# One level of Strassen's scheme in both products of a SwiGLU channel mixer, with operand sums through DRAM

## The chip, the core and the metric

The kernel runs on one core of a Trainium2 chip. The metric is device time in microseconds for one execution. The profile comes from one execution taken by the hardware profiler.

## What is computed

An encoder block: two token mixers (a state space model and a long convolution) beside each other, merged by gates, then a channel mixer. One sequence of 1024 tokens, 1024 channels, 2816 hidden channels in the channel mixer, all in float32. The part that matters here is the end:

```python
    merged = gate[:, :, 0] * y_a + gate[:, :, 1] * y_b
    x = x + g1[:, None, :] * (merged @ w_out[i])

    h = _modulate(_rmsnorm(x, norm2_g[i]), sh2, sc2)
    gu = h @ ffn_w_gu[i]
    x = x + g2[:, None, :] * ((jax.nn.silu(gu[..., :D_FF]) * gu[..., D_FF:]) @ ffn_w_down[i])
return _rmsnorm(x, final_g)
```

## The kernel before

Every large product is done in three matmuls. `split` (L134) makes from a float32 tile a rounded part on ACT (a cast, L135) and the rest on DVE or POOL (L136), and `mm3` (L139) adds high x high, high x low and low x high into one bank (L144, L145, L146). A row of the profile with one of these lines says nothing of the place; the tile's name does.

The channel mixer is the last stage. `emit_out` (L1348) multiplies the merged branches by `w_out` for two halves of 512 tokens (`th`), adds to `x1`, takes sums of squares on ACT, and for each half makes the second norm: `inv_rms` on DVE, four diagonal blocks `dg` (L1039), one matmul that spreads them to a row (`rrow`, L1384), 32 transposes (`xT`, L1390), and the scaled and shifted result, split, as `h2T`.

`emit_ffn` (L1408) then goes over the hidden channels in tiles of 128, `FF` = 22 for the gate and 22 for the up half, in four blocks of 6, 6, 6 and 4. For each it loads two weight tiles (`load_w`, L1043: 512 KB, cast on ACT, rest on POOL), does 48 matmuls of 512 columns for each (`gu`), applies Silu on ACT, multiplies on DVE and splits into `act`. After a block it multiplies by the matching rows of `ffn_w_down`: for the first three blocks in quarters of 256 columns (`dn`), for the last in halves of 512 (`dnl`). Each result is scaled by `g2` and added to `x1` on DVE (L1417, L1418). In the last block each tile of 128 tokens is finished at once: a sum of squares on ACT (L1011), the product with `final_g` on POOL (L1473), `inv_rms` on DVE and ACT, a scaling on ACT (L1480) and the store.

What an engine does next is fixed when the program is built: a scheduler puts the instructions of each engine in a row, and each engine works its row in order. All loads and stores of this stage are issued by SP, also in order. A tile from a pool with `bufs` buffers waits for the last reader of the buffer's former content.

## Time and profile before

| | |
|---|---|
| time, median of 3 runs | 1825.1 us (1824.79 to 1826.29) |
| the profiled execution: its time | 1826.97 us |
| the profiled execution: its span | 1825.2 us, 23002 instructions |
| PE busy | 1648.7 us (90%) |
| DVE busy | 1066.9 us (58%) |
| ACT busy | 593.6 us (33%) |
| POOL busy | 746.3 us (41%) |
| DMA | 194.38 MB, mean 106 GB/s |

Busy times are unions over the span of the core. PE and PEld (the load of the stationary operand) overlap. A matmul's own duration in the profile is longer than the distance to the next one, because matmuls are pipelined: what one costs in a row of them is the distance of two starts. Times are counted from the first instruction; the channel mixer's first matmul starts at 1070.03 us.

### The profile page before, as it was taken

The page shows a single profiled execution, that of the slowest core. Times are in us where ns is not written, and L with a number is a line of the kernel's source. Part 1 is how long each engine was busy: PE and PEld are TensorE (multiplying, and loading weights), DVE is VectorE, ACT ScalarE, POOL GpSimd, SP SyncE. Part 2 cuts the span into 40 slices and gives each one's busy share as a digit, 9 for nine tenths or more (in the row PEclk, how much of TensorE's full clock was granted, in tenths as well). Part 3 has the DMA queues.
Part 4 walks back from the last instruction along what each step waited for, and adds up shares of the span by engine and source line. Part 5 has one row for each costly group of instructions (what it writes and reads, how often), then busy time and mean ns, then how long its engine had stood idle before and what let it go on. Part 6 is the DMA issues. An engine that isn't in the chain of part 4 may idle for free.

```text
span 1825.2 us, 23002 instructions
## 1 busy us (share of the span) xinstructions
PE 1648.7 (90%) x8700; PEld 1402.7 (77%) x8700; DVE 1066.9 (58%) x1548; ACT 593.6 (33%) x1037; POOL 746.3 (41%) x509
## 2 busy tenths in 40 slices
PE   6778988998687899998699999999999999999996
PEld 2667767876566777776579997899888998899885
DVE  6889789788999727889877751122211231114127
ACT  5755455443233254222133532110121011110125
POOL 2356545258865347678621222222222222222234
PEclk9898999999888999999899999999999999999998
DMA  9445732433221267754258311111211121112112
GB/s 324 120 132 176 208 110 89 158 89 96 59 74 49 82 178 260 227 175 125 87 164 280 122 53 55 49 40 43 58 47 46 36 58 58 41 36 64 47 53 92
DMA packets 212946, 194.38 MB, mean 106 GB/s; under 512 B 23783, under 2 KB 174143, under 8 KB 211395
## 3 DMA queue, kind: packets, MB, share of 16 engines
q1 hardware_dynamic: 212356, 190.50, 33.8%
q0 software_dynamic: 480, 2.42, 0.4%
q8 instruction: 68, 1.11, 0.3%
q14 instruction: 42, 0.34, 0.1%
HBM read 149.91 MB, written 42.96 MB: 106 GB/s over the span
## 4 chain that ended last, share of the span: by engine, by line
PE 43%; DVE 3%; DMA 2%; ACT 1%; issue 1%; POOL 0%; ACTq 0%; DVEq 0%
PE gu L144 9%; PE gu L145 9%; PE gu L146 9%; PE dn L144 4%; PE dn L146 4%; PE dn L145 4%; DMA wof<-in_w_out_dram 1%; PE wop L144 1%; PE wop L145 1%; PE wop L146 1%; DVE x L1418 1%; DMA gb<-gates 0%; DVE wol L136 0%; DVE ss L1022 0%; PE br L144 0%
## 5 line engine op out<-in xcount | busy, mean ns | idle before, releaser
L136 POOL TENSOR_TENSOR wl<-wf,wh 128x1024 fp32r<-128x1024 f32 (+1 forms) x126 | 285.8, 2269 | 696.5 <-ACT wh L135 667.9
L135 ACT CAST wh<-wf 128x1024 fp32r<-128x1024 f32 (+1 forms) x126 | 118.5, 941 | 607.3 <-issue 191.2
L144 PE MATMUL gu<-h2T,wh 128*128 128x512 f32 x704 | 273.9, 391 | 3.4 <-ACT silu L1432 2.8
L145 PE MATMUL gu<-h2T,wh 128*128 128x512 f32 x704 | 275.0, 391 | 0.0
L146 PE MATMUL gu<-h2T,wl 128*128 128x512 f32 x704 | 274.7, 390 | 0.0
L1433 DVE TENSOR_TENSOR silu<-gu,silu 128x1024 f32<-128x1024 f32 x22 | 26.9, 1224 | 371.8 <-PE gu L146 365.5
L144 PE MATMUL pj<-hT,wh 128*128 128x512 f32 x480 | 197.8, 412 | 9.6 <-ACT cva L1180 8.9
L146 PE MATMUL pj<-hT,wl 128*128 128x512 f32 x480 | 195.7, 408 | 3.0 <-POOL wl L136 3.0
L145 PE MATMUL dn<-wl,act 128*128 128x256 f32 x576 | 162.8, 283 | 0.0
L146 PE MATMUL dn<-wh,act 128*128 128x256 f32 x576 | 162.8, 283 | 0.0
L144 PE MATMUL dn<-wh,act 128*128 128x256 f32 x576 | 161.8, 283 | 0.0
L144 PEld LDWEIGHTS gu<-h2T,wh 128*128 128x128 f32 x704 | 132.4, 188 | 31.4 <-ACT silu L1432 3.2
L146 PEld LDWEIGHTS gu<-h2T,wl 128*128 128x128 f32 x704 | 132.7, 188 | 27.5
L145 PEld LDWEIGHTS gu<-h2T,wh 128*128 128x128 f32 x704 | 132.7, 188 | 27.3
L144 PEld LDWEIGHTS pj<-hT,wh 128*128 128x128 f32 x480 | 95.1, 198 | 28.9 <-ACT cva L1180 9.6
L1417 DVE TENSOR_TENSOR tmp<-dn,g 128x256 f32<-128x256 f32 x96 | 35.9, 414 | 134.7 <-PE dn L146 134.7
L146 PEld LDWEIGHTS pj<-hT,wl 128*128 128x128 f32 x480 | 94.7, 197 | 22.9 <-POOL wl L136 3.8
L145 PEld LDWEIGHTS dn<-wl,act 128*128 128x128 f32 x576 | 110.7, 192 | 0.1
L146 PEld LDWEIGHTS dn<-wh,act 128*128 128x128 f32 x576 | 110.7, 192 | 0.0
L144 PEld LDWEIGHTS dn<-wh,act 128*128 128x128 f32 x576 | 110.1, 192 | 0.1
L145 PE MATMUL pj<-hT,wh 128*128 128x512 f32 x256 | 105.3, 411 | 0.0
L145 PE MATMUL pj<-lT,wh 128*128 128x512 f32 x224 | 90.4, 404 | 0.0
(411 smaller groups left out, 3732.4 us busy)
## 6 DMA issues: line engine op xcount, KB each, us to landing
wf<-in_ffn_w_gu_dram SPq DMA_DIRECT2D x44, 512.0 KB
wf<-in_w_in_dram SPq DMA_DIRECT2D x36, 512.0 KB
ada<-in_ada_w_dram SPq DMA_DIRECT2D x48, 256.0 KB
x<-in_x_dram SPq DMA_DIRECT2D x16, 512.0 KB
kt<-kspec SPq DMA_DIRECT2D x32, 256.0 KB
wof<-in_w_out_dram SPq DMA_DIRECT2D x16, 512.0 KB
wf<-in_ffn_w_down_dram SPq DMA_DIRECT2D x16, 512.0 KB
kspec<-kt SPq DMA_DIRECT2D x28, 256.0 KB
```

The lines of the kernel that those rows point to most:

```text
L135: E.nc.scalar.copy(hi, src)
L136: (lo_eng or E.nc.vector).tensor_tensor(out=lo, in0=src, in1=bc(hi), op=ALU.subtract)
L144: E.nc.tensor.matmul(out=out, lhsT=lh, rhs=rh, start=first, stop=False, skip_group_check=shared)
L145: E.nc.tensor.matmul(out=out, lhsT=lh, rhs=rl, start=False, stop=False, skip_group_check=shared)
L146: E.nc.tensor.matmul(out=out, lhsT=ll, rhs=rh, start=False, stop=last, skip_group_check=shared)
L1417: V.tensor_tensor(out=tmp, in0=acc, in1=E.g2[:, cs], op=ALU.mult)
L1418: V.tensor_tensor(out=x1[t][:, cs], in0=x1[t][:, cs], in1=tmp, op=ALU.add)
L1433: V.tensor_tensor(out=s, in0=pts[1], in1=s, op=ALU.mult)
```

## The change

Both products of the channel mixer are computed with seven block products in place of eight, in Winograd's form of Strassen's scheme. For the first, the stationary operand is the weight (gate above up, in two halves of the 1024 input channels) and the moving one is `h2T` (two halves of channels by two halves of tokens). For the second, the stationary operand is the activation (two halves of tokens by two halves of hidden channels) and the moving one `ffn_w_down`.

`emit_out` ends without the second half's norm; it stores `x1` to DRAM (`E.x1d`). `emit_norm2_end` makes that half's norm and the moving operands B22, T1, T2, T3, T4 of the first product (sums and differences on DVE, each split). `emit_gu` makes 11 passes `j`, each over the hidden tiles `j` and `j + 11`. For each tile, `weights` loads gate and up (`wg`, `wu`) and makes S1 to S4 on DVE, each split into `op`; `gate` is a generator of seven steps, one block product of 12 matmuls each, with results read out of the banks between them; two such generators run in turn. At the end of a pass DVE makes the four sums of the activations that the second product needs, and SP stores seven tiles of 256 KB to DRAM (`E.ad`).

`emit_down` has seven products over 11 `j` each. For each `j` it loads one A tile (`af`, a ring of 4) and one to three tiles of `ffn_w_down` (`bf`, a ring of 8; `t2` has tiles of its own), makes the T operands on DVE, and splits both into `dop`, a ring of 25. Four tiles of 128 tokens take each pair in turn (12 matmuls); in the last product, S4 by B22, all 11 pairs are made first and each tile runs through (33 matmuls). Results are put together on DVE, `x1` is loaded again (`y`), and the end of each tile is as before. PSUM is now one pool of eight banks for the stage.

```diff
-            ss = op.tile([P, 12], F32, tag="ss", name="ss2", bufs=2)
-            V.tensor_reduce(out=ss[:, 0:4], in_=sq, op=ALU.add, axis=mybir.AxisListType.X)
-            dg = diagonals(E, op, "dg", inv_rms(E, ss, 4))
...
+            for i in range(4):
+                nc.sync.dma_start(out=E.x1d[4 * th + i], in_=xs[i])
+            if th:
+                return sq
+            row = norm2_rows(E, rooms(op), ps, "n2", sq)
             for k in range(8):
...
-                hi, lo = E.hT[k, th] = [E.actT.tile([P, 512], F32R, tag="a", name="h2T") for _ in range(2)]
...
-                nc.scalar.activation(out=hi, in_=h, func=ACTF.Identity, bias=shift)
-                V.scalar_tensor_tensor(out=lo, in0=h, scalar=shift, in1=bc(hi), op0=ALU.add, op1=ALU.subtract)
+                h = E.actT.tile([P, 512], F32, tag="a", name="h2")
+                norm2(E, h, xs, k, row, ps, "n2")
+                E.h[k, 0] = h
+                hl = [E.actT.tile([P, 512], F32R, tag="a", name="h2T") for _ in range(2)]
+                split(E, h, *hl)
+                E.B["B11" if k < 4 else "B21"].append(hl)
...
+
+def strassen_a(TT, a11, a12, a21, a22, s1, s2, s3, s4):
+    TT(out=s1, in0=a21, in1=a22, op=ALU.add)
+    TT(out=s2, in0=s1, in1=a11, op=ALU.subtract)
+    TT(out=s3, in0=a11, in1=a21, op=ALU.subtract)
+    TT(out=s4, in0=a12, in1=s2, op=ALU.subtract)
...
+    for k in range(8):
+        h = room("h2", [P, 512])
+        norm2(E, h, x1[4:8], k, row, ps, "b")
+        h2.append(h)
+        if k < 4:
+            t1 = tmp()
+            V.tensor_tensor(out=t1, in0=h, in1=E.h[k, 0], op=ALU.subtract)
+            E.B["T1"].append([mine(), mine()])
+            split(E, t1, *E.B["T1"][k])
+    close()
+    pool = more()
+    for i in range(4):
+        at = (lambda: pool.tile([P, 512], F32R, tag="a", name="h2T")) if i < 2 else mine
+        b22, t3, t2, t4 = h2[i + 4], tmp(), tmp(), tmp()
+        V.tensor_tensor(out=t3, in0=b22, in1=h2[i], op=ALU.subtract)
+        V.tensor_tensor(out=t2, in0=t3, in1=E.h[i, 0], op=ALU.add)
+        for n, src, eng in (("B22", b22, GP), ("T3", t3, V), ("T2", t2, V), ("T4", None, V)):
+            if src is None:
+                src = t4
+                V.tensor_tensor(out=t4, in0=E.h[i + 4, 0], in1=t2, op=ALU.subtract)
+            hl = [at(), at()]
...
+        g = E.wp.tile([P, 8, P], F32, tag="wf", name="wg", bufs=2)
+        up = fp.tile([P, 8, P], F32, tag="wu", name="wu", bufs=2)
+        load(g, P * f)
+        load(up, (FF + f) * P)
...
+        split(E, g, gh, gl, nc.gpsimd)
+        four = lambda h, l, o=0: [(h[:, o + k], l[:, o + k]) for k in range(4)]
+        A["A11"], A["A12"] = four(gh, gl), four(gh, gl, 4)
+        g1, g2, u1, u2 = g[:, 0:4], g[:, 4:8], up[:, 0:4], up[:, 4:8]
+
+        def put(n, src):
+            t = fp.tile([P, 2, 4, P], F32R, tag="op", name="op", bufs=6)
+            split(E, src, t[:, 0], t[:, 1])
+            A[n] = four(t[:, 0], t[:, 1])
+
+        new = lambda: fp.tile([P, 4, P], F32, tag="ws", name="ws", bufs=3)
+        sub = lambda out, a, b: V.tensor_tensor(out=out, in0=a, in1=b, op=ALU.subtract)
+        s1, s2, s4, s3 = new(), new(), new(), new()
+        V.tensor_tensor(out=s1, in0=u1, in1=u2, op=ALU.add)
+        put("S1", s1)
+        sub(s2, s1, g1)
+        sub(s4, g2, s2)
+        put("S4", s4)
...
+        sub(s3, g1, u1)
+        put("S3", s3)
+        put("A22", u2)
...
+        go(X, "A11", "B11", True)
+        p1 = u("p1")
+        nc.scalar.copy(p1, X)
+        yield
...
+        go(Y, "S2", "T2", True)
+        g2 = u("g2")
+        V.tensor_tensor(out=g2, in0=Y, in1=p1, op=ALU.add)
+        V.tensor_tensor(out=g2, in0=Z, in1=g2, op=ALU.add)
+        nc.scalar.activation(out=g2, in_=g2, func=ACTF.Silu)
+        yield
+        go(Y, "S3", "T3", False)
+        a2 = u("a2")
+        V.tensor_tensor(out=a2, in0=Y, in1=p1, op=ALU.add)
...
+        go(Y, "A22", "T4", False)
+        a1 = u("a1")
...
+    for j in range(FH):
+        E.act = []
+        two = [gate(weights(f)) for f in (j, j + FH)]
+        for _ in range(7):
+            for g in two:
+                next(g)
+        (a11, a21), (a12, a22) = E.act[0:2], E.act[2:4]
+        S = [u("S") for _ in range(4)]
+        strassen_a(V.tensor_tensor, a11, a12, a21, a22, *S)
+        for n, t in zip(("A11", "A12", "A22", "S1", "S2", "S3", "S4"), [a11, a12, a22] + S):
+            nc.sync.dma_start(out=E.ad[n][j], in_=t)
...
+    nc.sync.dma_start(out=g2, in_=E.g2d.to_broadcast([P, L]))
+    nc.sync.dma_start(out=fg, in_=d["final_g"].rearrange("(a c) -> a c", a=1).to_broadcast([P, L]))
...
+    def operand(src, eng):
+        t = fp.tile([P, 2, 512], F32R, tag="op", name="dop", bufs=25)
+        split(E, src, t[:, 0], t[:, 1], eng)
+        return t[:, 0], t[:, 1]
+
+    def a(n, j):
+        t = fp.tile([P, 512], F32, tag="af", name="af", bufs=4)
+        nc.sync.dma_start(out=t, in_=E.ad[n][j])
+        return operand(t, V)
...
+        t = fp.tile([P, 512], F32, tag="bf", name="bf", bufs=8)
+        r = (FH * (i - 1) + j) * P
+        nc.sync.dma_start(out=t, in_=d["ffn_w_down"][0, r:r + P, 512 * (h - 1):512 * h])
...
+    def b(n, j):
+        if n[0] == "B":
+            t = load_b(int(n[1]), int(n[2]), j)
+        elif n == "T1":
+            t, o = load_b(1, 2, j), load_b(1, 1, j)
+            TT(out=t, in0=t, in1=o, op=ALU.subtract)
...
+        elif n == "T2":
+            t = t2[j] = fp.tile([P, 512], F32, tag=f"t2{j}", name="t2")
+            r = (FH + j) * P
+            nc.sync.dma_start(out=t, in_=d["ffn_w_down"][0, r:r + P, 512:1024])
+            for m, op in ((2, ALU.subtract), (1, ALU.add)):
+                TT(out=t, in0=t, in1=load_b(1, m, j), op=op)
...
+        return operand(t, GP if j % 3 == 2 else V)
+
+    def product(out, na, nb, start, whole=False):
+
+        ops = []
+        for j in range(FH):
+            ops.append((a(na, j), b(nb, j)))
+            if not whole:
+                for t in range(4):
...
+                    (ah, al), rhs = ops[j]
+                    mm3(E, out[t], [(ah[:, r], al[:, r])], [rhs], start and j == 0, j == FH - 1, True)
+        for t in range(4):
+            if whole:
+                r = slice(P * t, P * t + P)
+                mm3(E, out[t], [(ah[:, r], al[:, r]) for (ah, al), _ in ops], [rhs for _, rhs in ops], start, True, True)
...
+    def done(t, h):
+        sum_sq(E, y[t, h], v("junk"), sq[:, t, h:h + 1])
+        GP.tensor_tensor(out=y[t, h], in0=y[t, h], in1=half(fg, h), op=ALU.mult)
...
+    X, Y = four(), four()
+    for t in product(X, "A11", "B11", True):
+        p1.append(v("p1"))
+        nc.scalar.copy(p1[t], X[t])
+    for t in product(Y, "S2", "T2", True):
+        u2.append(v("u2"))
+        TT(out=u2[t], in0=Y[t], in1=p1[t], op=ALU.add)
...
+    for t in product(Y, "S3", "T3", False):
+        u3.append(v("u3"))
+        TT(out=u3[t], in0=Y[t], in1=p1[t], op=ALU.add)
+        load_y(t, 1)
+        add(t, 1, u2[t], u2[t])
...
+    for t in product(X, "S4", "B22", False, True):
+        add(t, 1, X[t])
+        done(t, 1)
+        finish(t)
...
+            sq = emit_out(E, mm, x1, woA, last_gate)
         wo.close()
-        ps2 = pool(top, "dn", space=PSUM)
-        emit_ffn(E, mm, ps2, x1)
+        sm.close()
+        ps = pool(top, "ff", bufs=8, space=PSUM)
+        with ExitStack() as s0:
+            fp = pool(s0, "ffn")
+            emit_norm2_end(E, fp, ps, x1, sq, sx.close, lambda: pool(right, "T2", bufs=16, side="right"))
+            emit_gu(E, fp, ps)
+        ws.close()
+        right.close()
+        emit_down(E, pool(top, "down"), ps)
```

PE at the start of the channel mixer: `rrow` is the matmul that spreads the second half's norm, `xT` are its transposes, `gu` is the first product. Before:

```order
L144 MATMUL gu<-h2T,wh 128x512
L145 MATMUL gu<-h2T,wh 128x512
L1384 MATMUL rrow<-dg,ones 128x512
L1390 MATMUL xT_9179<-ident,x_7925 128x128
L1390 MATMUL xT_9179<-ident,x_7926 128x128
```

And now, where `wop` is the product with `w_out`:

```order
L146 MATMUL wop<-woh,mT 128x256
L1358 MATMUL rrow<-dg,ones 128x512
L1369 MATMUL xT_9218<-ident,x_7934 128x128
L1369 MATMUL xT_9218<-ident,x_7935 128x128
L1369 MATMUL xT_9218<-ident,x_7936 128x128
```

Before, 38 matmuls of `gu` stand between the last `wop` and `rrow`, and the transposes come in groups between others; now `rrow` and all 32 transposes follow the last `wop`, and `gu` comes after them.

DVE in the same place, now: `Ts` are the sums for T1 to T4, `h2T` the splits of them, `ws` the sums of the first tile's weights (L1512 is S1's), `op` their splits.

```order
L1469 TENSOR_TENSOR Ts_9380<-Ts_9379,h2_8577 128x512
L136 TENSOR_TENSOR h2T_9389<-Ts_9379,h2T_9388 128x512
L1473 TENSOR_TENSOR Ts_9381<-h2_8577,Ts_9380 128x512
L1512 TENSOR_TENSOR ws_9409<-wu_9402 128x512
L136 TENSOR_TENSOR h2T_9393<-Ts_9380,h2T_9392 128x512
L136 TENSOR_TENSOR h2T_9398<-Ts_9381,h2T_9397 128x512
L1510 TENSOR_TENSOR ws_9410<-ws_9409,wg_9401 128x512
L136 TENSOR_TENSOR op_9414<-ws_9409,op_9414 128x512
```

S1 of the very first tile stands behind all sums of the moving operands but the last two splits.

SP between the two products, now: `adS2` to `adS4` are stores of the last pass, `af` and `bf` the first loads of the second product.

```order
L1572 DMA adS2_75<-S_12522 128x512
L1572 DMA adS3_76<-S_12523 128x512
L1572 DMA adS4_77<-S_12524 128x512
L1583 DMA g2r_12544<-g2d_70 128x1024
L1584 DMA fg_12545<-in_final_g_dram 128x1024
L1596 DMA af_12557<-adA11_71 128x512
L1602 DMA bf_12562<-in_ffn_w_down_dram 128x512
L1596 DMA af_12579<-adA11_71 128x512
```

Where before the weight tiles of `emit_ffn` followed one another through the whole stage, the second product's first load now stands behind the last store of the first.

## Rows read from the trace of the kernel before

**Rows 1.** The page, the chain that ended last: shares by line

```profile
PE gu L144 9%; PE gu L145 9%; PE gu L146 9%; PE dn L144 4%; PE dn L146 4%; PE dn L145 4%; DMA wof<-in_w_out_dram 1%; PE wop L144 1%; PE wop L145 1%; PE wop L146 1%; DVE x L1418 1%; DMA gb<-gates 0%; DVE wol L136 0%; DVE ss L1022 0%; PE br L144 0%
```

**Rows 2.** Timeline, start of the mixer: start, duration, engine, line, what

```profile
1070.03 0.39 PE L144 MATMUL gu<-h2T,wh 128*128 128x512 f32 x1
...
1073.19 0.88 DVE L1039 TENSOR_SCALAR dg<-ident,ss 128x128 f32<-128x128 f32 x4
...
1078.66 1.02 PE L1384 MATMUL rrow<-dg,ones 128*128 128x512 f32 x2
...
1080.33 0.75 DVE L1399 SCALAR_TENSOR_TENSOR hk<-xT,mod,rrow 128x512 f32<-128x512 f32 x1 [6.26 <-ACT rrow L1386]
```

**Rows 3.** Timeline, end of the kernel, PE and DVE

```profile
1809.53 0.39 PE L146 MATMUL dnl<-act 128*128 128x512 f32 x1
...
1811.38 0.68 DVE L1417 TENSOR_TENSOR tmp<-dnl,g 128x512 f32<-128x512 f32 x1
...
1814.70 0.68 DVE L1417 TENSOR_TENSOR tmp<-dnl,g 128x512 f32<-128x512 f32 x1
1815.42 0.69 DVE L1418 TENSOR_TENSOR x<-x,tmp 128x512 f32<-128x512 f32 x1
```

**Rows 4.** Busy time in the mixer's stretch, selected by tile: gu, dn, dnl

```profile
1070.00:1809.60 739.60, 482.74 (x2112) 396.98 (x2112) 26.93 (x22) 22.30 (x22) 1.00 0.16 48
...
1070.00:1809.60 739.60, 207.83 (x1728) 207.75 (x1728) 35.86 (x96) 1.00 0.16 48
...
1070.00:1809.60 739.60, 43.36 (x192) 36.05 (x192) 9.64 (x14) 1.00 0.16 48
```

**Rows 5.** Timeline of PE after its one gap in `gu`, and at its steady pace

```profile
1099.26 0.50 PE L144 MATMUL gu<-h2T,wh 128*128 128x512 f32 x1 [2.79 <-ACT silu L1432]
...
1101.44 0.63 PE L144 MATMUL gu<-h2T,wh 128*128 128x512 f32 x1
...
1104.43 0.52 PE L145 MATMUL gu<-h2T,wh 128*128 128x512 f32 x1
...
1105.26 0.39 PE L145 MATMUL gu<-h2T,wh 128*128 128x512 f32 x1
...
1109.79 0.39 PE L144 MATMUL gu<-h2T,wh 128*128 128x512 f32 x1
```

**Rows 6.** Stretches: PE, PEld, DVE, ACT, POOL busy, granted clock, DMA share, GB/s

```profile
1100.00:1110.00 10.00, 9.39 (x34) 7.63 (x35) 2.56 (x2) 1.19 (x2) 2.37 (x1) 0.83 0.37 105
1110.00:1212.00 102.00, 102.00 (x457) 84.74 (x456) 14.07 (x9) 18.90 (x19) 22.21 (x10) 1.00 0.15 44
```

**Rows 7.** The chain in order of time: start, duration, what; eight transposes

```profile
1079.68 0.87 PE xT L1390 x8
```

**Rows 8.** Groups by shape, from 1000 on: count, busy, mean ns, idle before

```profile
L136 POOL TENSOR_TENSOR wl<-wf,wh 128x1024 fp32r<-128x1024 f32 x58 | 139.9, 2413 | 487.2 <-ACT wh L135 487.2
...
L1473 POOL TENSOR_TENSOR yo<-x,fg 128x512 f32<-128x512 f32 x16 | 20.7, 1291 | 19.7 <-DVE ss L1021 10.3 <-DVE x L1418 7.5 <-DVE ss L1022 1.8
L1418 DVE TENSOR_TENSOR x<-x,tmp 128x512 f32<-128x512 f32 x16 | 15.7, 983 | 0.5
...
L135 ACT CAST wh<-wf 128x512 fp32r<-128x512 f32 x12 | 7.4, 620 | 68.9 <-PE dn L146 42.1 <-issue 26.7
```

**Rows 9.** Timeline, POOL and DVE at the same time in the merge

```profile
930.99 1.62 POOL L136 TENSOR_TENSOR wl<-wf,wh 128x512 fp32r<-128x512 f32 x1 [4.50 <-ACT wh L135]
931.38 1.78 DVE L1341 TENSOR_TENSOR gb<-gb,ya 128x512 f32<-128x512 f32 x1
```

**Rows 10.** The chain in order of time: two 256 KB transfers

```profile
962.29 8.15 DMA gb<-gates
...
1000.29 3.49 DMA acc<-acc
```

**Rows 11.** Stretches with the densest transfers, columns as in rows 6

```profile
950.00:975.00 25.00, 22.32 (x119) 18.69 (x119) 17.69 (x26) 6.88 (x11) 1.96 (x2) 1.00 0.83 287
...
1000.00:1025.00 25.00, 25.00 (x210) 24.88 (x209) 15.64 (x28) 11.13 (x27) 6.14 (x4) 1.00 0.58 184
```

More of the change, by code (lines that the diff above doesn't have):

```diff
@@ L1356, in emit_out @@
             xs = x1[4 * th:4 * th + 4]
[L1357 removed]
+            sq = E.cp.tile([P, 4, 4], F32, name="sq")
             for q in range(4):
@@ L1379, in emit_out @@
                     between()
-            ss = op.tile([P, 12], F32, tag="ss", name="ss2", bufs=2)
-            V.tensor_reduce(out=ss[:, 0:4], in_=sq, op=ALU.add, axis=mybir.AxisListType.X)
-            dg = diagonals(E, op, "dg", inv_rms(E, ss, 4))
-            pt = ps.tile([P, 512], F32, tag="n2", name="rrow")
-            nc.tensor.matmul(out=pt, lhsT=E.ones, rhs=dg.rearrange("p a b -> p (a b)"), start=True, stop=True)
-            row = op.tile([P, 512], F32, tag="rrow", name="rrow")
-            nc.scalar.copy(row, pt)
@@ new lines, with emit_norm2_end @@
+FF = 22
+FH = FF // 2
+def strassen_a(TT, a11, a12, a21, a22, s1, s2, s3, s4):
[3 more added lines that the diff above has]
+    TT(out=s4, in0=a12, in1=s2, op=ALU.subtract)
+def emit_norm2_end(E, fp, ps, x1, sq, close, more):
+    nc = E.nc
+    V, GP = nc.vector, nc.gpsimd
+    room = lambda tag, shape: fp.tile(shape, F32, tag="u", name=tag, bufs=NU)
+    row = norm2_rows(E, room, ps, "b", sq)
+    h2 = []
+    mine = lambda: E.actT.tile([P, 512], F32R, tag="a", name="h2T")
+    tmp = lambda: fp.tile([P, 512], F32, tag="ws", name="Ts", bufs=3)
+    for k in range(8):
[9 more added lines that the diff above has]
+    pool = more()
+    for i in range(4):
+        at = (lambda: pool.tile([P, 512], F32R, tag="a", name="h2T")) if i < 2 else mine
[7 more added lines that the diff above has]
+            hl = [at(), at()]
+            split(E, src, *hl, eng)
+            E.B[n].append(hl)
@@ new lines, in gate, with go @@
+    def gate(A):
+        def go(out, a, b, start):
+            mm3(E, out, A[a], E.B[b], start, True, True)
+        X, Y, Z = bank(), bank(), bank()
+        go(X, "A11", "B11", True)
+        p1 = u("p1")
+        nc.scalar.copy(p1, X)
+        yield
+        go(X, "A12", "B21", False)
+        s = u("s1")
+        nc.scalar.activation(out=s, in_=X, func=ACTF.Silu)
+        yield
+        go(Z, "S1", "T1", True)
+        p5 = u("p5")
+        nc.scalar.copy(p5, Z)
+        yield
+        go(Z, "S4", "B22", False)
+        yield
+        go(Y, "S2", "T2", True)
[3 more added lines that the diff above has]
+        nc.scalar.activation(out=g2, in_=g2, func=ACTF.Silu)
+        yield
+        go(Y, "S3", "T3", False)
+        a2 = u("a2")
+        V.tensor_tensor(out=a2, in0=Y, in1=p1, op=ALU.add)
+        V.tensor_tensor(out=a2, in0=a2, in1=p5, op=ALU.add)
+        V.tensor_tensor(out=a2, in0=a2, in1=g2, op=ALU.mult)
+        yield
+        go(Y, "A22", "T4", False)
+        a1 = u("a1")
+        V.tensor_tensor(out=a1, in0=Y, in1=p1, op=ALU.add)
+        V.tensor_tensor(out=a1, in0=a1, in1=s, op=ALU.mult)
+        E.act += [a1, a2]
+        yield
@@ L1498, in hybrid_block @@
         E.acc = D("acc", [4, P, L])
+        E.x1d, E.g2d = D("x1d", [8, P, L]), D("g2d", [1, L])
+        E.ad = {n: D("ad" + n, [FH, P, 512]) for n in ("A11", "A12", "A22", "S1", "S2", "S3", "S4")}
+        E.h, E.B = {}, {n: [] for n in ("B11", "B21", "B22", "T1", "T2", "T3", "T4")}
         E.ya = D("ya", [8, P, L])
```

186 lines of the change are left out of this document (98 added, 88 removed).

## The prediction

> **What bounds the kernel now.** First the chain that ended last [rows 1]: it runs through the matmuls of the channel mixer, `gu` and `dn`; no other engine has a large share in it. Then the mixer's own stretch. Its first `gu` matmul starts at 1070.03 [rows 2], its last `dnl` matmul at 1809.53 [rows 3], and the span ends at 1825.2. By the three rows that select a tile [rows 4] PE's busy time there is 482.74 + 207.83 + 43.36 = 733.9 us of those 739.9: PE is full. The spacing of starts gives the price of one matmul: 20 steps from 1105.26 to 1109.79, so 0.2265 us for 512 columns [rows 5]; the 256-column ones cost 207.83/1728 = 0.120 us [rows 4]. In the same stretch DVE works 14 of 102 us, POOL 22, and the transfers move 44 GB/s [rows 6]. So there is room beside PE, and fewer matmul columns are worth their full price, as long as the new work of DVE and of the transfers stays under PE's shorter time.
>
> **What goes.** Before: 2112 `gu` x 0.2265 + 1728 `dn` x 0.120 + 192 `dnl` x 0.2265 = 478.4 + 207.4 + 43.5 = 729.3 us. After: `emit_gu` issues 11 passes x 2 gates x 7 products x 12 = 1848 matmuls, `emit_down` 7 products x 11 x 4 x 3 = 924, all of 512 columns: 418.6 + 209.3 = 627.9 us. The gain is 101.4 us at most: an eighth of the columns, and 6% on the half-width ones.
>
> **What comes at the start.** PE had 38 `gu` matmuls to do while DVE made `dg` from the last sums of squares. In the new order `rrow` and all 32 transposes stand ahead of the first `gu` matmul, so PE waits from 1070.0 until `dg` is done at 1073.19 + 0.88 [rows 2]: 4.1 us. `rrow` and the transposes cost 1.02 [rows 2] + 4 x 0.87 [rows 7] = 4.5 us, as before. Then 48 matmuls on `A11`, `A12` need only what is ready and last 10.9 us, until 1089.5. The next product needs S1. DVE takes S1's first step (L1512) after 4 `h2` steps and 30 sums, differences and splits for T1 to T4. It can start 1.67 us after `rrow` does, the distance from 1078.66 to 1080.33 [rows 2], at about 1075.8. With 0.75 us for each of the 4 [rows 2] and 0.69 for each 128x512 tensor-tensor alone [rows 3], that is 3.0 + 31 x 0.69 = 24.4 us, to 1100.2. But POOL works in this stretch too: four products with the row, four splits of B22, two weight splits of 2.41 us [rows 8]. Beside a POOL operation of 1.62 us a DVE one took 1.78 instead of 0.69 [rows 9], 1.1 us more; ten such meetings add up to 11 us. So S1 comes between 1100 and 1111; I take 1108, nearer the upper end, since POOL's list is long, and a cast of 0.62 [rows 8]. PE waits 19.2 us here (11 to 22). The rest of this first pass has 27.2 us of PE and some 40 DVE steps of 0.69 = 27.6 us: 3 us more (0 to 8).
>
> The first trace row on this sharing is the 1.78 us one. The Trainium skill, "SBUF — State Buffer", section "SBUF: two separate sides", calls the pair of ports that DVE and GpSimd share an exclusive lock, the loser waiting for the whole instruction; by it each meeting would cost DVE a whole POOL operation, 1.3 us and not 1.1, and the first wait would be some 2 us longer. The trace's 1.1 is below that and decides.
>
> **The ten further passes.** A pass has 168 matmuls, 38.1 us. DVE has 36 steps of 0.69 = 24.8 us, and two POOL splits of 2.41 us beside it; ACT has two casts of 1024 and some 18 of 512 columns, about 13 us at 0.62 for 512 [rows 8]. Both fit. Bank `Y` is read by DVE between two products into it; the other gate's product, 12 x 0.2265 = 2.7 us, is the cover. I take 4 us for all ten (0 to 20: two late reads in each pass).
>
> **Between the products.** SP issues the first load of `emit_down` behind the last store of pass 10, and behind `g2r` and `fg`. From PE's last `gu` matmul: three DVE steps (2.1 us), then about 2.4 MB of stores and loads up to the first pair, then a cast and a split (1.3 us). The transfer is bounded by 3.5 us, a lone 256 KB [rows 10], and by 2.4 MB at 287 GB/s [rows 11], 8.3 us. I take the second, since all is queued at once: 12 us (7 to 15).
>
> **The down stage.** Up to its last pair SP loads 214 x 256 KB + 1 MB = 57.2 MB. At 287 GB/s [rows 11] that is 199 us beside 209.3 us of PE: close, but under. DVE has about 244 tensor-tensors (77 splits of A, 56 of B, 55 sums and differences of weights, 56 on results): 168 us at 0.69, and 37 POOL operations of 1.29 us [rows 8] that cost it up to 1.1 us each, 41 us. Together 209, again PE's time; the ring of 25 `dop` tiles lets the operands run up to 12 pairs (33 us) ahead, which evens out the heavy products (S2·T2, S3·T3, S1·T1). I take 8 us of waits (0 to 30).
>
> **Clock and end.** After a gap of 2.79 us [rows 5] the granted clock fell to 0.83 of full over 10 us [rows 6]: between 1101.44 and 1104.43 seven matmuls took 0.427 us each, the spacing at 1.2 GHz, and cost 1.4 us. I take 4 us for the gaps above (1.4 to 8). The end: from the last tile's `tmp` at 1814.70 to 1825.2 [rows 3], 10.5 us behind the last matmul. Before, DVE, ACT and POOL ran 3.3 us per tile against PE's 2.7, so they trailed PE by 4.8 us there; now a tile of the last product has 33 matmuls, 7.5 us, and nothing trails.
>
> **Sum.** 1070.0 + 4.1 + 4.5 + 418.6 + 19.2 + 3 + 4 + 12 + 209.3 + 8 + 4 + 10.5 = 1767.2 us of span, 58 below 1825.2. The profiled execution took 1826.97 and becomes 1769; the median of the runs, 1825.1, stands beside the span, so the time is 1767.
>
> **The rivals.**
>
> *DVE sets the down stage.* If its 244 steps go at the mean of `x<-x,tmp` beside POOL, 0.983 us [rows 8], they take 240 us, with four `finish` of 3.3 us 253, against 217 in the sum: 1767 + 36 = 1803. For it: POOL splits every third B operand. Against: most steps meet no POOL operation, which is busy 48 us.
>
> *The loads set the down stage* (the one that ends slower). A ring of four `af` tiles turns once per load, cast and split. At 8.15 us for a load, the longest on the chain before [rows 10], that is 9.5/4 = 2.4 us a pair against PE's 2.7. It becomes the bound from a landing of about 9.6 us, and eats the whole gain (66 us over 77 pairs, 3.6 us a pair) from 13 us on. At the 184 GB/s of 1000 to 1025 [rows 11], 57.2 MB take 311 us: 1767 + 94 = 1861. For it: SP is one queue in order, and each load waits for a split of DVE. Against: where the transfers were wanted they ran at 287 GB/s with 0.83 of the engines busy [rows 11].
> Here a page speaks against the change: the Trainium skill, "DMA: Bandwidth & Descriptors", section "Rules for kernel authors", asks for 1 MiB per transfer, and its table under "Bandwidth" has 138 GB/s at 64 KB, 341 at 1 MB; at an estimated 138 for these 256 KB loads the stage would take over 400 us. The trace's 287 GB/s, reached with loads of 256 and 512 KB in flight together, disagrees.
>
> *PE waits at every read of `Y`.* If DVE's queue is behind by more than the cover of 2.7 us in every pass, each of 44 reads shows 0.69 us and a handover, say 1.4 us by two DVE steps: 62 us, 1767 + 58 = 1825, no change.
>
> *All is covered.* S1 at 1100 (8 less), no waits in down (8), none in the passes and the first pass's rest (7), a switch of 7 us (5): 1739.
>
> **Chances.** The forecast (1748 to 1792) 0.57; DVE in down (1792 to 1815) 0.15; all covered (1735 to 1748) 0.13; loads in down 0.09; waits at `Y` 0.06, half of it slower, a third the same. A measurement of this kernel tells about 0.2%, 3.6 us, from no change. Faster 0.86, same 0.02, slower 0.12. The range that leaves out the last two is 1738 to 1812.
>
> **What would show it.** Right: PE's 1848 and 924 matmuls at 0.2265 us; one wait of PE of some 19 us after 48 `gu` matmuls with DVE as the releaser; 11 to 13 us between last `gu` and first `dn`; passes of 38 to 39 us; a down stage of 209 to 225 us. Wrong: gaps in every pass, or PE waiting through the down stage on `dop` with DVE idle (loads) or full (DVE).

## The result, and the profile after

The changed kernel takes 1768.3 us (median of 4 runs, 1766.17 to 1775.56) against 1825.7 before: the ratio is 0.969, 95% interval 0.966 to 0.972. A second set of runs of the same kernel gave 1767.4 (1765.02 to 1769.97), ratio 0.968 (0.966 to 0.969). The forecast was 1767, so it was right in sum. It was not right term by term, and that is the more useful part of what follows.

The page of the first profile after the change: span, PE, DVE and POOL busy, then the chain that ended last by line, which answers to [rows 1].

```profile
span 1773.8 us, 21889 instructions
PE 1566.3 (88%) x7440; PEld 1287.4 (73%) x7440; DVE 1333.7 (75%) x1944; ACT 722.8 (41%) x1331; POOL 708.7 (40%) x484
PE gu L145 8%; PE gu L144 8%; PE gu L146 8%; POOL dop L136 1%; DMA bf<-in_ffn_w_down_dram 1%; DMA wof<-in_w_out_dram 1%; DMA af<-adA 1%; DMA af<-adS 1%; DMA y<-x1d 1%; DVE dop L136 1%; PE dn L144 1%; ACT dop L135 1%; DVE h2T L136 1%; PE dn L145 1%; PE dn L146 1%
```

PE is still what bounds the mixer: `gu` leads the chain. DVE has gone from 58% to 75% of the span; the transfers from 194 to 264 MB.

This first profile comes from the slowest of the four executions. The second profile (1767.3 us of span) stands near the median, so the reading goes by it. Its waits of PE from 1050 us on: who waited for whom, total us, times, longest:

```profile
PE gu L144 <- ACT op L135: 13.4, 1, 13.4
PE dn L144 <- ACT dop L135: 13.2, 1, 13.2
PE rrow L1358 <- DVE dg L1356: 3.9, 1, 3.9
PE gu L146 <- DVE op L136: 0.5, 1, 0.5
PE gu L144 <- ACT p L1531: 0.3, 1, 0.3
```

Three waits make up nearly all of it: for the first S1 (`op`), between the products (`dop`), and for `dg`. In the first profile the same three are there, and 3.9 us more of waits in the second product, by which it is slower. The stretches of the second profile, columns as in [rows 6]:

```profile
1070.00:1082.00 12.00, 8.07 (x42) 6.60 (x41) 6.54 (x17) 4.94 (x11) 2.44 (x2) 0.72 0.54 153
...
1093.00:1107.00 14.00, 0.58 (x2) 0.47 (x2) 14.00 (x23) 8.32 (x15) 5.81 (x2) 0.62 0.00 0
1107.00:1120.00 13.00, 12.35 (x41) 8.90 (x41) 12.74 (x17) 5.58 (x9) 7.10 (x2) 0.75 0.41 122
1120.00:1528.00 408.00, 408.00 (x1757) 330.76 (x1756) 239.26 (x374) 126.95 (x204) 45.80 (x19) 1.00 0.30 94
1528.00:1542.00 14.00, 0.94 (x5) 0.43 (x3) 4.23 (x7) 1.14 (x2) 0.00 (x0) 0.69 0.84 267
1542.00:1560.00 18.00, 17.85 (x69) 14.60 (x70) 9.90 (x15) 8.38 (x15) 2.58 (x2) 0.86 1.05 386
1560.00:1740.00 180.00, 179.94 (x794) 148.72 (x793) 155.00 (x228) 91.15 (x170) 61.72 (x29) 1.00 0.78 267
```

From 1093 to 1107 PE works 0.6 us of 14 while DVE has not one free moment; from 1120 to 1528 PE is full and DVE 59% busy; from 1560 to 1740 PE is full again, DVE 86%. The granted clock is 1.00 in the full stretches and between 0.62 and 0.86 around the three waits.

The terms of the sum beside what this profile shows (us; the third column is worked out from the starts of the first and last matmul of each stage, which are 1074.36 for `rrow`, 1081.12 and 1528.56 for `gu`, 1542.15 and 1754.08 for `dn`):

| term | forecast | measured |
|---|---|---|
| up to PE's wait for `dg` | 1070.0 | 1070.4 |
| wait for `dg` | 4.1 | 3.9 |
| `rrow` and 32 transposes | 4.5 | 6.8 |
| 1848 `gu` | 418.6 | 429.5 |
| wait for S1 | 19.2 | 13.9 |
| rest of the first pass, ten further passes | 7 | 0 |
| between the products | 12 | 13.4 |
| 924 `dn` | 209.3 | 209.5 |
| waits in the down stage | 8 | 0 |
| clock and handovers (4.2 in `gu`, 2.6 in `dn`) | 4 | 6.8 |
| behind the last matmul | 10.5 | 13.0 |
| sum | 1767.2 | 1767.2 |

Seven terms were 20.5 us too low together and four 20.5 us too high.

### The profile page after: what moved, and what is told of

It reads as the page before. It is cut to its first block, busy times and chain, and to the rows that moved or that the text cites. A ratio compares the mean times of both kernels' runs of the same rounds, so it can differ in the third digit from the quotient of the medians.

```text
span 1773.8 us, 21889 instructions
## 1 busy us (share of the span) xinstructions
PE 1566.3 (88%) x7440; PEld 1287.4 (73%) x7440; DVE 1333.7 (75%) x1944; ACT 722.8 (41%) x1331; POOL 708.7 (40%) x484
## 5 line engine op out<-in xcount | busy, mean ns | idle before, releaser
L136 POOL TENSOR_TENSOR wl<-wf,wh 128x1024 fp32r<-128x1024 f32 (+1 forms) x56 | 130.3, 2326 | 162.6 <-ACT wh L135 131.1
L144 PE MATMUL gu<-h2T,op 128*128 128x512 f32 x440 | 174.9, 397 | 13.9 <-ACT op L135 13.9
L136 POOL TENSOR_TENSOR wl<-wg,wh 128x1024 fp32r<-128x1024 f32 x22 | 53.8, 2446 | 317.3 <-ACT wh L135 317.3
L145 PE MATMUL gu<-h2T,op 128*128 128x512 f32 x440 | 174.8, 397 | 0.0
L146 PE MATMUL gu<-h2T,op 128*128 128x512 f32 x440 | 169.7, 396 | 0.5 <-DVE op L136 0.5
L144 PE MATMUL dn<-dop 128*128 128x512 f32 x308 | 114.9, 395 | 14.7 <-ACT dop L135 14.7
L135 ACT CAST op<-ws 128x512 fp32r<-128x512 f32 x88 | 54.3, 620 | 178.4 <-PE gu L146 171.7
L145 PE MATMUL dn<-dop 128*128 128x512 f32 x308 | 121.6, 395 | 2.1 <-DVE dop L136 2.1
L146 PE MATMUL dn<-dop 128*128 128x512 f32 x308 | 121.0, 393 | 0.0
L144 PEld LDWEIGHTS gu<-h2T,op 128*128 128x128 f32 x440 | 83.3, 189 | 34.3 <-ACT op L135 15.0
L136 POOL TENSOR_TENSOR dop<-bf,dop 128x512 fp32r<-128x512 f32 x18 | 42.9, 2383 | 150.6 <-ACT dop L135 72.2
L146 PEld LDWEIGHTS gu<-h2T,op 128*128 128x128 f32 x440 | 83.5, 190 | 20.9 <-DVE op L136 1.3
L145 PEld LDWEIGHTS gu<-h2T,op 128*128 128x128 f32 x440 | 83.5, 190 | 19.3
L136 DVE TENSOR_TENSOR dop<-af,dop 128x512 fp32r<-128x512 f32 x77 | 58.6, 762 | 31.6 <-ACT dop L135 31.3
L144 PEld LDWEIGHTS dn<-dop 128*128 128x128 f32 x308 | 58.5, 190 | 27.7 <-ACT dop L135 15.6
L135 ACT CAST dop<-af 128x512 fp32r<-128x512 f32 x77 | 47.8, 621 | 67.9 <-DMA af<-adA 53.4
```

The costliest lines, as they stand in the source:

```text
L135: E.nc.scalar.copy(hi, src)
L136: (lo_eng or E.nc.vector).tensor_tensor(out=lo, in0=src, in1=bc(hi), op=ALU.subtract)
L144: E.nc.tensor.matmul(out=out, lhsT=lh, rhs=rh, start=first, stop=False, skip_group_check=shared)
L145: E.nc.tensor.matmul(out=out, lhsT=lh, rhs=rl, start=False, stop=False, skip_group_check=shared)
L146: E.nc.tensor.matmul(out=out, lhsT=ll, rhs=rh, start=False, stop=last, skip_group_check=shared)
```

## The experiments

The edits are small, so each is told by the few lines that differ. "The changed kernel" is the one of the diff above; where a stage is compared, it is with its second profile. `thin`, `edge_24_nopool`, `edge_72_rows` and `edge_8_inner` have one execution each (1597.9, 1764.7, 1753.0 and 1766.2 us), and what is said of them is read inside a stage of the trace, not from these times.

### The changed kernel once more

> The changed kernel once more, unaltered. In its first profile a gu matmul cost 0.2324 us (starts from 1170.99 to 1210.03, 168 matmuls) and a dn matmul 0.2267, and that execution took 1775.6 us where three others took 1766 to 1769. Theory A: the slower spacing belongs to that one execution; then this profile, if its time is near 1767, shows gu at about 0.2267 and a first product some 10 us shorter. Theory B: it belongs to the program; then gu is at 0.232 again whatever the time, and the 8 us between the executions are elsewhere.

Measured: 1767.4 us, and `gu` again at 0.2324 us a matmul in each pass (39.0 us for 168), `dn` at 0.2267. Theory B: the spacing belongs to the program. The 6.5 us between the two profiled spans lie nearly all in the second product: 217.8 against 211.9 us from first to last `dn`.

### The pad ahead of the moving operands

By the program's addresses, which no trace shows, the stationary tiles of `gu` start at 192 modulo 256 bytes in the changed kernel and the moving ones at 64; before, both started at 64. A tile that only takes up room stands ahead of the moving operands, and its width says where these start. The change took it from 424 floats to 40. That is 1536 bytes, six times 256, so this line alone leaves the moving tiles where they were modulo 256; it is the stationary ones that came to start elsewhere. The experiment makes the pad 8, so that the moving tiles follow by 128 bytes.

```diff
-            pool(right, "edge", side="right").tile([P, 40], F32, name="edge")
+            pool(right, "edge", side="right").tile([P, 8], F32, name="edge")
```

> The pad tile ahead of the moving operands is 8 floats wide and no longer 40, so that all tiles of that side of SBUF lie 128 bytes elsewhere; nothing else differs. By the program's addresses a stationary tile of gu starts at 192 modulo 256 bytes and a moving one at 64 in the changed kernel; before the change both started at 64, and the tiles of dn all start at 192. Theory A (stationary and moving tiles that start at unlike places modulo 256 slow the pairs of weight load and matmul): gu falls from 0.2324 to 0.2267 us a matmul, 1848 x 0.0057 = 10.5 us, and the time to 1755 to 1759. Theory B (the slower spacing comes from the order of the products, or from what DVE and ACT do beside them): gu stays at 0.232 and the time at 1767.

> Two edits in stretches that the trace tells apart. First, the pad is 24 floats: moving tiles of gu start at 128 modulo 256 bytes against 192 of the stationary ones, 64 apart where the changed kernel has them 128 apart. If only an equal start gives 0.2267 us, gu shows something slower here too (0.229 to 0.233); if 64 apart does no harm, 0.2267. Second, the splits of the second product that POOL made are made by DVE. Theory A (DVE sets the stage only where it shares with POOL): DVE works some 14 us more, dn stays within 4 us of 212, with no wait on POOL. Theory B (POOL relieves DVE where it is the bound): dn grows by 5 to 14 us, with waits on DVE's dop.

> Two edits in stretches that the trace tells apart. First, the pad is 72 floats: moving tiles of gu start at 192 modulo 512 bytes and stationary ones at 448, equal modulo 256 and 256 apart modulo 512; in edge_8 both start at 448 modulo 512. If equal starts modulo 256 are enough, gu is at 0.2267 us a matmul; if they must agree modulo 512, at 0.232 or so. Second, the two rows g2 and final_g (512 KB each as written) are loaded behind the second product's first pairs and no longer ahead of them. Theory A (the gap of 13.6 us between the products is partly transfers that run together, 1 MB at 388 GB/s): it shrinks by 2 to 3 us, to 11. Theory B (SP's issues in order and one transfer's own latency set it): by the two issues, 1 us.

Measured, `edge_8`: 1759.5 us (1755.91 to 1763.77), 7.8 under the changed kernel; the first product is 10.2 us shorter, the gap behind it 1.3 us longer. `edge_24_nopool` and `edge_72_rows` have a second edit each, of which more below. The stretch of 1200 to 1400 us, selected by the tile `gu`: length, then PE's busy time with its count. The changed kernel, pad 40:

```profile
1200.00:1400.00 200.00, 200.00 (x862) 162.17 (x861) 28.20 (x41) 16.05 (x30) 1.00 0.32 102
```

pad 8:

```profile
1200.00:1400.00 200.00, 200.00 (x884) 165.66 (x883) 29.59 (x43) 16.00 (x30) 1.00 0.33 104
```

pad 24:

```profile
1200.00:1400.00 200.00, 200.00 (x859) 161.15 (x858) 27.53 (x40) 16.04 (x30) 1.00 0.32 102
```

pad 72:

```profile
1200.00:1400.00 200.00, 200.00 (x884) 165.62 (x883) 29.81 (x44) 16.00 (x30) 1.00 0.32 102
```

In the same 200 us, PE full and the granted clock at 1.00 in all four, 884 matmuls go through where stationary and moving tiles start at the same place modulo 256 bytes, and 859 to 862 where they start 64 or 128 apart, all by the program's addresses. A pass takes 38.1 us with the pad of 8 and 39.0 with 40; the whole first product 437.2 against 447.4 us. Starts 256 apart (pad 72) do no harm. In all of these runs the fast place of the moving tiles is 192; that it is the equal start that counts, and not that place, rests on the kernel before, with both at 64 and 0.2265 us [rows 5]. So Theory A holds, and the mis-sized `gu` term was not a property of Strassen's scheme but of where its operands lie.

### The wait for S1: order or amount

`s1_early` runs the first three products' emission, with all weight operands of the first two tiles, ahead of the loop over T2 to T4; `early_s` writes S1 and S4 of these tiles ahead of the norm (the comments are not in the code):

```diff
+    early()        # early_s: here, ahead of norm2_rows: S1, S4 of tiles 0 and 11
     row = norm2_rows(E, room, ps, "b", sq)
...
     close()
     pool = more()
+    early()        # both: the first three products (s1_early: and all weight operands)
     for i in range(4):
         at = (lambda: pool.tile([P, 512], F32R, tag="a", name="h2T")) if i < 2 else mine
```

> The first pass's weight operands (S1 to S4 and A22 of tiles 0 and 11) and its first three products are written ahead of the sums T2, T3, T4 of the moving operands; nothing is added or left out. Theory A (the forecast's: PE waits 14 us for S1 because DVE has 30 sums and splits ahead of it): the wait after the 48 matmuls on A11 and A12 falls from 13.7 us to under 2, the 13 matmuls at half clock behind it (2.5 us) go too, and T2 to T4 are ready before PE wants them since the next pass's A11 products can go first: 12 to 17 us faster. Theory B (DVE's total work up to the end of the first pass sets the time, whatever comes first): the wait comes back at S2 times T2 or A22 times T4, and the gain is under 4 us. Theory C (the wait is for the weight loads or the ring of three sums): nothing changes.

> S1 and S4 of the first two tiles are written ahead of the second half's norm, so that DVE makes what it can of them while it waits for dg, rrow and the transposes; S2, S3 and A22 follow T1, and T2 to T4 come last. In s1_early the one wait of 13.4 us became eight of 0.6 to 2.2 us, together 10 with their spacing, and the first product shortened by 3 us only. Theory A (DVE's sum of work until the first pass ends sets its time, so only work that moves into DVE's idle time helps): 4 to 5 of DVE's steps move into that time, 3 us, and the first product is 5 to 8 us shorter than the changed kernel's 447.4. Theory B (order alone decides, and s1_early had a bad one): all waits of the first pass go, 12 us or more. Theory C: as s1_early, 3 us.

PE's waits in `s1_early`:

```profile
PE gu L144 <- ACT p L1540: 3.3, 2, 2.0
PE gu L144 <- DVE g L1546: 1.5, 1, 1.5
PE gu L144 <- ACT op L135: 1.4, 2, 1.0
PE gu L144 <- ACT h2T L135: 1.0, 1, 1.0
```

and in `early_s`:

```profile
PE gu L144 <- ACT h2T L135: 4.3, 1, 4.3
...
PE gu L144 <- DVE g L1549: 1.4, 1, 1.4
```

`s1_early` took 1761.3 us (1759.77 to 1763.01), `early_s` 1765.5 (1763.10 to 1768.51). These times hold more than the edit: the point at which `gu` begins lay at 1077.6 and 1081.7, and over all the runs here between 1076.4 and 1082.5. The stage itself is the better measure: from first to last `gu` 444.3 and 443.6 us against 447.4. The one wait of 13.4 us is gone in both, but most of it came back in pieces, at reads of results (`p`, `g`) and at T2 (`h2T`). In `early_s` the spacing of `gu` was 0.2333, which costs 1848 x 0.0009 = 1.7 us; without that its gain is 5.5 us, within Theory A's 5 to 8.

Where the gain comes from shows in the first pass and the second, from the first matmul of each to that of the next (the third busy time is DVE's). The changed kernel:

```profile
1081.12:1138.38 57.26, 42.89 (x171) 33.08 (x170) 54.26 (x71) 31.66 (x53) 22.44 (x9) 0.85 0.16 46
1138.38:1177.42 39.04, 39.04 (x169) 31.65 (x168) 22.14 (x36) 12.52 (x20) 4.82 (x2) 1.00 0.33 102
```

`s1_early`, then `early_s`:

```profile
1077.61:1131.78 54.17, 45.56 (x172) 33.81 (x170) 50.30 (x64) 31.36 (x53) 17.46 (x10) 0.91 0.13 39
1131.78:1170.82 39.04, 39.04 (x170) 31.65 (x168) 26.98 (x44) 13.14 (x21) 4.83 (x2) 1.00 0.36 115
...
1081.70:1133.49 51.79, 44.89 (x171) 33.84 (x170) 46.60 (x62) 30.63 (x51) 16.68 (x10) 0.90 0.18 48
1133.49:1172.69 39.20, 39.20 (x169) 31.53 (x168) 26.28 (x42) 13.12 (x21) 4.81 (x2) 1.00 0.33 105
```

DVE fills the first pass in all three. With the edits 7 and 9 of its 71 steps lie outside this pass; its work there falls by 4.0 and 7.7 us, the pass itself by 3.1 and 5.5. Most of these steps now run in the second pass, where DVE was busy 22.1 of 39.0 us. So the gain goes with what moves into time in which DVE stood idle, ahead of the pass or behind it; the rest of the wait is only spread.

### What lies under PE

```diff
-        E.nc.tensor.matmul(out=out, lhsT=lh, rhs=rh, start=first, stop=False, skip_group_check=shared)
-        E.nc.tensor.matmul(out=out, lhsT=lh, rhs=rl, start=False, stop=False, skip_group_check=shared)
+        if shared:
+            E.nc.tensor.matmul(out=out, lhsT=lh, rhs=rh, start=first, stop=last, skip_group_check=shared)
+            continue
```

> Two of the three matmuls of every block product in gu and dn are left out (high x low and low x high), and all loads, casts, splits, sums and stores stay: 616 gu and 308 dn matmuls are left, 140 and 70 us. The time of each stage is then that of what lies under PE. Theory A (the forecast's numbers): a pass of gu takes what DVE needs, 25 to 30 us against 38; the stage of dn takes the longer of DVE's 209 us and the loads' 57.2 MB, 199 us at 287 GB/s and 155 at the 370 that the first profile shows: 180 to 215 us against 218, so PE is the bound by a little only. Theory B (DVE at 0.76 us a step with no cost of sharing): 170 to 185 us in dn. Theory C (loads in order behind the rings set the stage, hidden only by chance): dn stays within 5 us of 218.

Two stretches of this kernel, in the first and in the second product:

```profile
1140.00:1370.00 230.00, 162.14 (x535) 114.81 (x533) 224.75 (x339) 112.22 (x187) 47.68 (x18) 0.82 0.48 153
1400.00:1540.00 140.00, 87.46 (x232) 55.43 (x232) 124.02 (x184) 72.75 (x135) 60.79 (x21) 0.73 0.88 309
```

With two thirds of the matmuls gone, a later pass takes 24.7 us (mean of the nine between the starts of passes 1 and 10, 1123.5 and 1345.5), just under Theory A's 25 to 30, and DVE is busy 224.75 of 230 us: DVE is the next bound of the first product, 13.4 us a pass behind the forecast's 38.1 of PE. From first to last `dn` it is 179.2 us against 211.9, with DVE 89% busy and the transfers at 0.88 of their engines: two bounds close together, 33 us behind PE. That is Theory B's range for the second product (170 to 185), just under A's. The rivals in which DVE or the loads set the down stage needed 36 and 94 us more than the sum; the run puts the next bound 33 us away on the other side.

### Between the products

`act_stores` and `act_stores_nopool` move the last pass's stores; the second also takes POOL's splits away.

```diff
-            nc.sync.dma_start(out=E.ad[n][j], in_=t)
+            (nc.scalar if j == FH - 1 else nc.sync).dma_start(out=E.ad[n][j], in_=t)
...
-        return operand(t, GP if j % 3 == 2 else V)
+        return operand(t, V)
```

> The seven stores of the last pass of gu are issued by ACT's queue and no longer by SP's, so that the first loads of the second product have no store ahead of them on SP. Theory A (the switch of 12.9 us is a chain: three DVE steps, SP's issues in order, then the transfers): the first loads are issued at PE's last gu matmul or earlier instead of 5 us behind it, and the gap shrinks by 3 to 6 us, with the time. Theory B (the transfers themselves, some 2.4 MB at 388 GB/s, set it): the gap shrinks by under 1.5 us. Theory C: the loads wait for the memory of gu's tiles, not for the queue, and nothing changes; or ACT, held by the last store, makes the casts later and the gap grows by 1 to 2 us.

> The stores of the last pass on ACT's queue, as in act_stores, and no POOL split in the second product. In act_stores the gap between the products fell from 13.6 to 9.7 us, and yet the kernel was 12 us slower: PE waited 12.4 us once for a split of POOL's, three of which took 22.7 us together while DVE worked without a pause. Theory A (the loss is POOL held up by DVE, and only that): the wait is gone, the gap of 9.7 stays, and the time is 3 to 5 us under the changed kernel's, 1762 to 1764. Theory B (the loss comes from loads that run earlier and collide): dn stays at 220 or more, with waits on DVE or on loads in POOL's place.

How the gap runs in the changed kernel (timeline, SP's queue, DVE and ACT):

```profile
1531.99 0.69 DVE L1441 TENSOR_TENSOR S<-a,S 128x512 f32<-128x512 f32 x1
1533.12 0.41 SPq L1583 DMA_DIRECT2D g2r<-g2d  x1
1533.62 0.44 SPq L1584 DMA_DIRECT2D fg<-in_final_g_dram  x1
1534.16 0.41 SPq L1596 DMA_DIRECT2D af<-adA  x1
...
1540.81 0.62 ACT L135 CAST dop<-af 128x512 fp32r<-128x512 f32 x1 [18.83 <-DMA af<-adA]
```

The last matmul of `gu` starts at 1528.56. The first load is issued 5.6 us later, behind the stores and the two rows, and is there 6.6 us after its issue. With the rows loaded later (`edge_72_rows`) the same two lines read:

```profile
1518.28 0.39 SPq L1594 DMA_DIRECT2D af<-adA  x1
...
1521.52 0.62 ACT L135 CAST dop<-af 128x512 fp32r<-128x512 f32 x1 [14.19 <-DMA af<-adA]
```

3.2 us from issue to cast, and the gap (last start of `gu` to first of `dn`) is 9.4 us, against 13.6 in the changed kernel and 14.9 in `edge_8`. That is more than Theory A's 2 to 3 us: without 1 MB of rows ahead of it the first load is issued 1.0 us sooner behind the last `gu`, and is there 3.4 us sooner after its issue. Part of this is paid back: the second product, into which the rows were moved, takes 214.9 us against 211.8 in `edge_8`, with 1.5 us of waits for `dop`.

With the stores on ACT's queue the gap is 9.7 us, as Theory A had it, though the first load is still issued 2.6 us behind the last `gu` and not at it. But `act_stores` took 1779.1 us (1777.72 to 1780.18), 11.7 more than the changed kernel. The place, first POOL's timeline, then PE's:

```profile
1569.87 22.69 POOL L136 TENSOR_TENSOR dop<-t,dop 128x512 fp32r<-128x512 f32 x3 [7.65 <-ACT dop L135]
...
1589.24 0.79 PE L145 MATMUL dn<-dop 128*128 128x512 f32 x1 [12.44 <-POOL dop L136]
```

Three splits that take 1.3 us each alone took 22.7 together, the first of them 19.3, and PE waited 12.4 us for one of them. In that stretch DVE's instructions follow one another at 0.60 us with no gap (DVE's busy time is the third, POOL's the fifth):

```profile
1570.00:1588.00 18.00, 6.80 (x30) 5.28 (x29) 18.00 (x30) 11.20 (x20) 18.00 (x1) 0.80 1.03 379
```

The split ended at 1589.2, 1.1 us after DVE's first pause, which came at 1588.05. `act_stores_nopool` has no such wait: 1762.4 us (1758.26 to 1765.07), a gap of 9.4 us, first to last `dn` 212.2. Its Theory A holds.

Taking the splits from POOL costs little. Measured in `edge_24_nopool` between 1544 and 1752, DVE is busy 176.0 us against 171.5 in the changed kernel. By count it should be 21 x 0.69 = 14 us more; the other 10 do not show. That DVE no longer meets POOL there is the likely reason; it was not tried apart. First to last `dn` is 211.0 us, no longer than with POOL's help.

### The end

```diff
-    for t in product(X, "S4", "B22", False, True):
+    for t in product(X, "S4", "B22", False):
```

> The pad of 8 floats, no POOL split in the second product, and the last product (S4 by B22) with the four tiles of tokens inside each pair, as the other six have it, so that all four tiles end within 2.7 us of each other and not 7.5 us apart. Beside edge_24_nopool, whose last product runs tile by tile and whose tail is 9.0 us behind the last dn matmul. Theory A (DVE, ACT and POOL take 3.3 us a tile one after the other at the end, as at the end of the kernel before): the tail is 9 + 3 x 3.3 = 19 us, the product itself no shorter. Theory B (the tiles' ends overlap across the engines): 11 to 14 us.

The tail, from the last `dn` matmul's start to the end, was 18.5 us against 9.0 in `edge_24_nopool`: Theory A, 19. So running the last product tile by tile is worth 9.5 us, where POOL makes no splits. In the changed kernel itself the tail is 13.3. The first step of each of the last four tiles on DVE, in the changed kernel:

```profile
1744.80 0.67 DVE L1651 TENSOR_TENSOR tmp<-dn,g2r 128x512 f32<-128x512 f32 x1
...
1749.94 0.69 DVE L1651 TENSOR_TENSOR tmp<-dn,g2r 128x512 f32<-128x512 f32 x1
...
1754.25 0.68 DVE L1651 TENSOR_TENSOR tmp<-dn,g2r 128x512 f32<-128x512 f32 x1
...
1758.74 0.69 DVE L1651 TENSOR_TENSOR tmp<-dn,g2r 128x512 f32<-128x512 f32 x1
```

and of the first and the last two in `edge_24_nopool`:

```profile
1737.16 0.67 DVE L1651 TENSOR_TENSOR tmp<-dn,g2r 128x512 f32<-128x512 f32 x1
...
1746.63 0.69 DVE L1651 TENSOR_TENSOR tmp<-dn,g2r 128x512 f32<-128x512 f32 x1
...
1754.12 0.69 DVE L1651 TENSOR_TENSOR tmp<-dn,g2r 128x512 f32<-128x512 f32 x1 [2.90 <-PE dn L146]
```

In the changed kernel DVE takes the last tile 4.4 us after PE's last matmul (start 1754.08, one spacing long), since the tiles before it, and the finish of the product before, still run; without POOL's splits DVE is idle and waits for PE there. The lag is older than the last product's end: the first of the four steps comes 7.6 us later than in `edge_24_nopool`, while PE's last matmul differs by 0.4 us. All kernels that run the last product by tiles had a tail of 9.0 us without these splits and 12.4 to 13.4 with them (`thin` apart, whose matmuls are too few to compare). Whether POOL's queue or the row in which the scheduler put DVE's instructions makes the difference was not tried apart.

### All together

> Four edits together: the pad of 8 floats (edge_8), the last pass's stores on ACT's queue with no POOL split in the second product (act_stores_nopool), and S1 and S4 of the first tiles ahead of the norm (early_s). By the traces so far the edits touch different stretches: gu at 0.2267 us a matmul (10 us), a gap of 9.4 us between the products and a tail of 9.0 behind the last dn (8 us together), 4 us in the first pass. Theory A (they add): 1743 to 1748. Theory B (what one gives another takes, above all a first pass that gains nothing once its matmuls are shorter, since DVE sets it): 1749 to 1755.

> The same four edits with the order of s1_early in place of early_s: all weight operands of the first two tiles behind T1 and ahead of T2 to T4. In the first product s1_early gained 3.1 us and early_s 3.8 us, the latter at a slower spacing (0.2333 against 0.2324, 1.7 us). If the spacing is mended by the pad in both, best_early should be 2 to 3 us ahead of this one; if DVE's sum of work sets the first pass, within 1 us of it.

`best_early` takes 1744.8 us (1743.13 to 1747.66), 0.9555 of before (0.9538 to 0.9572), and beats both kernels; `best_s1` takes 1748.2 (1744.57 to 1753.21). The page of `best_early` and PE's waits in it:

```profile
span 1742.8 us, 21860 instructions
...
PE 1550.8 (89%) x7440; PEld 1283.5 (74%) x7440; DVE 1328.3 (76%) x1965; ACT 724.3 (42%) x1331; POOL 652.6 (37%) x463
```

```profile
PE dn L144 <- ACT dop L135: 11.4, 1, 11.4
PE gu L144 <- ACT h2T L135: 4.3, 1, 4.3
PE rrow L1358 <- DVE dg L1356: 3.9, 1, 3.9
```

The time is in Theory A's range. In the first product the edits add to the tenth of a us: 431.7 us against 447.4 is 15.7 less, and `edge_8` gained 10.2 and `early_s`, at equal spacing, 5.5. The second product (211.3) and the tail (9.0) are as in the runs with one edit. The gap is not: 11.8 us, where `act_stores_nopool` had 9.4 and `best_s1` has 9.6; in `best_early` the cast of the first `bf` starts 5.6 us after that load's issue, in `best_s1` 3.6. Why, the traces don't tell.

The two orders of the first pass differ by 0.9 us in the first product (431.7 and 432.6): within 1 us, as the theory that DVE's amount of work sets this pass has it, and with nearly the same number of DVE steps in it (61 and 62). The medians of the times are 3.4 us apart, in ranges that overlap, and the profile of `best_s1` is of its fastest execution; so the times do not settle it.

## Why the prediction was right, point by point

**PE bounds, the columns are worth their price: right.** 1848 and 924 matmuls were issued, PE is full in all passes but the first and through the down stage, and `thin` shows the next bound 13.4 us a pass and 33 us a stage behind.

**1848 x 0.2265: mis-sized, 10.9 us too low.** The spacing in [rows 5] is right for operands laid out as before the change. It was carried over as if it belonged to the shape alone. By the program's addresses the change left the operands 128 bytes apart modulo 256, and the step cost 0.2324. `edge_8` takes the whole error of the step away.

**The start: mechanism right, sizes off both ways.** PE waits for `dg` (3.9, forecast 4.1), and once, after 48 `gu` matmuls, for S1. Its wait was 13.9 us and not 19.2 (range 11 to 22). In the first profile S1's first step came at 1106.4 and PE could go on at 1107.75, the forecast's 1108.7 almost to the us, for reasons that cancel: DVE began 2.8 us later than forecast, and a step in a full row costs 0.60 us from start to start, not the 0.69 that one lasts. PE came to the wait later than forecast: `rrow` and the transposes now stand behind the wait for `dg`, ran at a mean granted clock of 0.64 of full (1074.36 to 1081.12) and cost 6.8 us, where the forecast had 4.5 from rows at full clock. So the clock term was put in the wrong place as well as too small.

**Rest of the first pass, ten further passes (7 us): nothing there.** After the wait DVE was ahead, and the cover of 2.7 us at each read of `Y` always held; the rival with 44 waits is out.

**Between the products (12): right in sum, 13.4.** The chain is 3.7 us of DVE's last steps (forecast 2.1), 1.5 of SP's issues (not in the sum), 6.6 of a load that shares the transfers with 1 MB that nobody needs yet (between the two bounds of 3.5 and 8.3, nearer the one taken), and 1.3 of a cast and a split.

**The down stage (8 us of waits): none in the second profile, 3.9 in the first, 12.4 in `act_stores`.** The loads ran at 386 GB/s at the start of the stage, where the sum had 287 from [rows 11]: a reading of what the transfers had been asked for, taken as what they can do. The Trainium skill, "DMA: Bandwidth & Descriptors", section "Rules for kernel authors", asks for 1 MiB a transfer for the highest rate; these loads are 256 KB each, many in flight, and 386 GB/s at a share of 1.05 of the engines disagrees, as the prediction had judged from 287.

**Behind the last matmul (10.5): 13.0.** "Nothing trails" was wrong: DVE trailed PE by 4.4 us. The step failed by looking only at the last product's own 7.5 us a tile; the finish of the product before it was still queued on DVE.

**DVE and POOL: the price per meeting was right, the rule drawn from it wrong.** A DVE step beside a POOL one costs some 1.1 us more, as in [rows 9]. From that the prediction took the exclusive lock of the Trainium skill ("SBUF — State Buffer", section "SBUF: two separate sides") to be disproved. The row does not disprove it: the DVE step began 0.39 us into POOL's and ended 0.55 us after it, as a step would that stood still for the 1.23 us that were left. The other side of it was not looked at: `act_stores` shows POOL standing for some 18 us beside 30 DVE steps without a pause, until DVE's first pause, which fits an engine locked out. Why POOL got no turn between two of these steps, no run tells. The sum had a price for DVE beside POOL and none for POOL beside DVE, nor for PE behind POOL. In the changed kernel PE shows no such wait; in `act_stores`, with the same work in a slightly different row, it cost 12.4 us.

So the time came out to the us because errors of 20 us each way met, by luck. The range, 1738 to 1812, was the part of the forecast that deserved to be right.

## What to carry to other kernels

When a change moves operands, the price of a matmul from the old trace holds only if stationary and moving tiles still start at like places; compare the addresses of both, before and after, and set a pad so that they agree. Where one engine does a stage's preparation without a pause, another order within it only spreads the wait; gain comes from work that moves into time in which that engine stood idle, before or after. Do not put work that PE waits for on POOL beside a DVE that has no gaps: here DVE did the same splits for a third of their price by count.
